# A two-layer encoder on one core: the order of the last products of a group of pairs, and which engine copies one of their sums

## The chip, the core and the metric

The kernel runs on one core of a Trainium2 chip. Its engines work beside each other, each through its own queue of instructions in a fixed order: TensorE (PE, with its weight loads shown as PEld) multiplies matrices and adds into PSUM; VectorE (DVE) and ScalarE (ACT) read and write PSUM and the on-chip memory SBUF; GpSimd (POOL) and SyncE (SP) only issue transfers here. An instruction waits until those whose results it reads, or whose data it overwrites, are done. The metric is the device time of one execution in microseconds (us).

## The reference

Two layers over 512 tokens and 16 learned ones (528 columns in the kernel, 512 in the last block), 1024 channels, in float32:

```python
for l in range(DEPTH):
    h = h + 0.5 * swiglu(rmsnorm(h, norm_gains[l, 0]),
                         ffn_w_gate[l, 0], ffn_w_up[l, 0], ffn_w_down[l, 0])
    h = h + mixer(rmsnorm(h, norm_gains[l, 1]), ...)
    h = h + 0.5 * swiglu(rmsnorm(h, norm_gains[l, 2]),
                         ffn_w_gate[l, 1], ffn_w_up[l, 1], ffn_w_down[l, 1])
return rmsnorm(h, final_norm)[:, N_META:]

def swiglu(x, w_gate, w_up, w_down):
    return (jax.nn.silu(x @ w_gate) * (x @ w_up)) @ w_down
```

The mixer (gated linear attention beside softmax attention) isn't touched by the change. The four `swiglu` blocks are, each with 2816 hidden channels.

## The kernel before, in words

**Two parts of each number.** Every matrix product is made in three: each operand is split into a high part (a cast to the type that TensorE multiplies fast) and a low part (what the cast left). High times high, high times low and low times high add up in PSUM. The high part of a block of weights is a cast on ScalarE (line 287), the low part a subtraction on VectorE (line 288). Activations are split likewise (lines 673 and 674 for the down products).

**Seven products for eight.** In the feed-forward blocks the products are made by a scheme of the Strassen kind: operands are cut in two each way, and seven products of sums and differences replace eight. They are named "1" to "7". Products 1, 6, 7 and 4 of a pair add up in one PSUM tile (X), product 2 has one of its own (Y), products 5 and 3 share a third (Z). "Pair" means two blocks of 128 hidden channels, with gate and up; there are 11 in a feed-forward block, in groups of 4, 4 and 3. One product of a pair is 24 matmuls of 264 columns (256 in the last block), all at line 598.

The running sum in X is read after each product, and the next one then adds on: ScalarE copies it out after products 1, 6 and 7 (`snapshot`, line 602); VectorE adds Y or Z to the copies (lines 608, 618, 625). `hidden` then multiplies by the norm's factor (line 642), applies the activation on ScalarE (line 444) and multiplies gate and up (line 652).

**A group's end.** Behind the last pair of each of the first two groups (pairs 3 and 7) the hidden channels of the group, four pairs of them, are multiplied by the down weights, again in seven products ("S" steps, `fast_down`, matmuls at line 712, sums added to the result `h` at line 720), for each of two halves of the output. Their operands are made from the four hidden quarters by `operand` (lines 673 and 674) and `difference` (line 678). As three of the four pairs are done early, the first operands are made in two steps ("O"): three quarters while the last pair is still at work, the last quarter behind it. So the first three down products of the first half have a part 1 (18 matmuls, for three pairs) and a part 2 (6, for the last pair). There are two such places in each of four blocks, eight in all.

**Weights.** They come through SP's queue in blocks of 128 x 1024 into three buffers, or for sums into others; products 3, 5, 6 and 7 need sums or differences of weight blocks, which are made by transfers of POOL's queue that add to what is there (line 208), by VectorE (line 256) or begin with a negated copy on ScalarE (line 203). `W.behind` keeps a cast of weights behind the last copy of a sum on ScalarE's queue. Blocks are fetched nine loads ahead and split three ahead, in the order of their use.

The order of the steps is written out in `ffn_steps`; a scheduler then places each engine's instructions, so that their order on an engine can differ a little from that of the code.

Of the kernel before, what the change touches and what calls it, by code (L numbers as in the profile page):

```python
# [14 lines left out]
ALU = mybir.AluOpType  # L15
AX = mybir.AxisListType

P = 128
# [22 lines left out]

GROUPS = (4, 4, 3)
FAST = 2
QUADS = 2
LATE = 5
HELD = 4
# [6 lines left out]
def ffn_steps(opening):  # L53

    steps, pair = [], 0
    for g, n in enumerate(GROUPS):

        ahead = g == 0  # L60
        begun = 0 < g <= FAST
        steps += [("P", p, c) for p in range(pair, pair + 1 + ahead) for c in "12"] * (not begun)
        early4 = (0, 1) if opening and ahead else ()
        steps += [("P", p, "4") for p in early4]
        steps += [("P", pair, c) for c in "65"] * (not begun)
        for i in range(n):
            p, more = pair + i, i + 1 < n
            early = [[("P", p + 1, "1")], [("P", p + 1, "2")]] if more else \
                [[("D", g, 0, 0, 2 * n - 2)], [("D", g, 1, 0, 2 * n - 2)]]
            if ahead and i == 0:  # L70
                early = [[], []]
            if not more and g < FAST:
                rest = [("S", g, 0, c, 2) for c in "125"]
                steps += [("O", g, 0), ("P", p, "7"), ("P", p, "4"), ("S", g, 0, "1", 1), ("P", p, "3")]
                steps += [("S", g, 0, c, 1) for c in "25"] + [("O", g, 1)] + rest
                turns = [("S", g, *t, 3) for t in zip(AB, "16273465734")]
                steps += turns[:6]
                for s, c in zip(turns[6:], "1265"):
                    steps += [s, ("P", p + 1, c)]
                steps.append(turns[-1])  # L80
                continue
            steps += early[0] + [("P", p, "7")] + early[1] + [("P", p, c) for c in "43" if c == "3" or p not in early4]
            if more:
                steps += [("P", p + 1, "6"), ("P", p + 1, "5")]
        if g >= FAST:
            steps += [("D", g, m, 0, 2 * n - 2) for m in range(2, HELD)]
            steps += [("D", g, m, 2 * n - 2, 2 * n) for m in range(HELD)]
            steps += [("D", g, m, 0, 2 * n) for m in range(HELD, KC)]
        pair += n
    return steps  # L90
# [238 lines left out]
def build(tc, ctx, xt, wts, win, par, w2, const, umask, out):  # L329
# [243 lines left out]
    def ffn(l, f, norm, done, following):  # L573
# [7 lines left out]
        def product_of_pair(p, product):  # L581
            kind = "s2" if p % 2 == 0 else "ss"
            st = made.setdefault(p, {})
            apart = product == "4" and "r" not in st
            where, begin = {"1": ("X", 1), "6": ("X", 0), "7": ("X", 0), "4": ("X", 0), "2": ("Y", 1), "5": ("Z", 1),
                            "3": ("Z", 0)}[product]
            if apart:
                where, begin = "W", 1
            if begin:
                st[where] = pair(kind == "s2")  # L590
            acc = st[where][:, :, :w]

            hi, lo = W.op((l, f), p, product, ahead=AHEAD_MADE - 1)
            at = PLACE[product]
            for k, (xh, xl) in enumerate(x):
                for j in range(2):
                    for i, (a, b) in enumerate(((hi, xh), (hi, xl), (lo, xh))):
                        TE.matmul(acc[:, j], a[:, j, k], b[:, at], start=bool(begin and k == 0 and i == 0),  # L598
                                  stop=k == len(x) - 1 and i == 2, skip_group_check=not begin)

            def snapshot(q):
                W.behind = S.copy(part(st, q), acc).ins  # L602

            if product == "1":
                st["c"] = [c_tile() for _ in range(2)]
                snapshot(0)
            elif product == "2":
                V.tensor_tensor(part(st, 0), part(st, 0), acc, ALU.add)
            elif product == "6":
                snapshot(1)  # L610
            elif apart:
                S.copy(part(st, 2), acc)
                st["apart"] = True
            elif product == "7":
                snapshot(3)
                if "apart" in st:
                    V.tensor_tensor(part(st, 2), part(st, 2), part(st, 3), ALU.add)
                V.tensor_tensor(part(st, 3), part(st, 3), st["Z"][:, :, :w], ALU.add)
                st["r"] = True
                if "apart" in st:  # L620
                    hidden(st, p, 1)
            elif product == "4":
                hidden(st, p, 1)
            elif product == "3":
                V.tensor_tensor(part(st, 1), part(st, 1), acc, ALU.add)
                hidden(st, p, 0)
# [121 lines left out]
        for i, step in enumerate(steps):  # L748
# [16 lines left out]
            elif step[0] == "O":  # L765
                g, last = step[1:]
                ks = slice(3, 4) if last else slice(0, 3)
                operands_of(g, ks, "215" if last else "125")
                difference(g, 0, 3, 0, ks)
                if last:  # L770
                    operand(g, "6")
# [599 lines left out]
```

## Time and profile before

| what | value |
|---|---|
| median of 3 runs | 2212.42 us (2210.72 to 2214.04) |
| the profiled execution | 2211.05 us |
| its span, first to last instruction | 2209.2 us |
| PE busy | 2162.4 us, 98% |
| VectorE busy | 1785.4 us, 81% |
| ScalarE busy | 1214.1 us, 55% |
| POOL busy | 101.8 us, 5% |
| granted TensorE clock, mean | 0.997 |

A row of a timeline has the start and the duration in us, the engine, the line, the operation, what is written and read, the shape, and a count where instructions follow each other; behind them, in brackets, the engine's idle time ahead of it and what ended it. A row of the view of waits has the waiting engine with its line, what it waited for, and the total in us, the number and the longest. A matmul's duration overlaps with the next one's, so distances are taken from start to start. The tile names are the program's: `ss` is a PSUM sum, `xc` an activation operand, `whi` and `wlo` the parts of a block of weights, `w`, `s` and `raw` blocks or sums of weights, `c` a pair's copies (or an operand of the down products), `g` a hidden quarter or an operand, `h` the result.

### The profile page before, as it was taken

The page shows a single profiled execution, that of the slowest core. Times are in us where ns is not written, and L with a number is a line of the kernel's source. Part 1 is how long each engine was busy: PE and PEld are TensorE (multiplying, and loading weights), DVE is VectorE, ACT ScalarE, POOL GpSimd, SP SyncE. Part 2 cuts the span into 40 slices and gives each one's busy share as a digit, 9 for nine tenths or more (in the row PEclk, how much of TensorE's full clock was granted, in tenths as well). Part 3 has the DMA queues.
Part 4 walks back from the last instruction along what each step waited for, and adds up shares of the span by engine and source line. Part 5 has one row for each costly group of instructions (what it writes and reads, how often), then busy time and mean ns, then how long its engine had stood idle before and what let it go on. Part 6 is the DMA issues. An engine that isn't in the chain of part 4 may idle for free.

```text
span 2209.2 us, 40079 instructions
## 1 busy us (share of the span) xinstructions
PE 2162.4 (98%) x16506; PEld 2070.2 (94%) x16506; DVE 1785.4 (81%) x2703; ACT 1214.1 (55%) x1779; POOL 101.8 (5%) x120
## 2 busy tenths in 40 slices
PE   7999999999999999999999999999999999999998
PEld 6999999989999999999999999999788888999997
DVE  7897978486886689889789979775879767997987
ACT  7544545344785555454575445453457836554543
POOL 1000000000000001000010000000000001000100
PEclk9999999999999999999999999999999999999999
DMA  9775753212113468666567757432121145776752
GB/s 268 189 204 160 191 152 106 82 49 68 49 39 122 114 167 205 190 182 187 162 163 186 207 164 191 143 110 77 49 84 51 42 133 152 198 202 181 189 165 67
DMA packets 87463, 311.41 MB, mean 141 GB/s; under 512 B 9712, under 2 KB 12144, under 8 KB 87280
## 3 DMA queue, kind: packets, MB, share of 16 engines
q1 hardware_dynamic: 68624, 245.53, 32.9%
q0 software_dynamic: 16704, 60.82, 15.8%
q8 instruction: 130, 2.13, 0.4%
q10 hardware_dynamic: 1952, 2.50, 0.4%
q14 instruction: 53, 0.43, 0.1%
HBM read 289.94 MB, written 2.10 MB: 132 GB/s over the span
## 4 chain that ended last, share of the span: by engine, by line
PE 81%; DVE 11%; ACT 4%; issue 2%; DMA 2%; SPq 0%; DVEq 0%; ACTq 0%
PE ss L598 37%; PE mm L465 13%; PE ss L712 11%; PE ss L465 10%; PE sm L465 2%; DVE wlo L288 2%; DMA w<-win 2%; PE sm L1074 1%; PE ss L1049 1%; DVE g L678 1%; ACT whi L287 1%; PE sm L1090 1%; DVE h L720 1%; PE ss L471 1%; PE sm L1091 1%
## 5 line engine op out<-in xcount | busy, mean ns | idle before, releaser
L598 PE MATMUL ss<-xc,whi 128*128 128x264 f32 (+1 forms) x4928 | 907.2, 285 | 15.5 <-ACT whi L287 7.4
L598 PEld LDWEIGHTS ss<-xc,whi 128*128 128x128 f32 x4928 | 767.2, 189 | 20.4 <-ACT c L602 8.4
L598 PE MATMUL ss<-xc,wlo 128*128 128x264 f32 (+1 forms) x2464 | 702.5, 285 | 8.8 <-DVE wlo L288 8.8
L598 PEld LDWEIGHTS ss<-xc,wlo 128*128 128x128 f32 x2464 | 466.5, 189 | 11.1 <-DVE wlo L288 10.9
L288 DVE TENSOR_TENSOR wlo<-w,whi 128x1024 fp32r<-128x1024 f32 (+1 forms) x337 | 408.1, 1217 | 63.4 <-ACT whi L287 63.2
L287 ACT CAST whi<-w 128x1024 fp32r<-128x1024 f32 (+1 forms) x337 | 350.0, 1050 | 163.3 <-PE ss L598 80.5
L465 PE MATMUL mm<-x,whi 128*128 128x264 f32 (+1 forms) x1712 | 384.6, 315 | 0.0
L465 PEld LDWEIGHTS mm<-x,whi 128*128 128x128 f32 x1712 | 278.3, 188 | 16.5 <-issue 1.0
L465 PE MATMUL mm<-x,wlo 128*128 128x264 f32 (+1 forms) x856 | 266.0, 315 | 0.0
L712 PE MATMUL ss<-g,whi 128*128 128x264 f32 (+1 forms) x1280 | 237.4, 284 | 0.0
L287 ACT CAST whi<-raw 128x1024 fp32r<-128x1024 f32 x126 | 132.3, 1050 | 163.4 <-PE mm L465 102.3
L602 ACT COPY c<-ss 128x528 f32<-128x528 f32 (+1 forms) x132 | 78.5, 594 | 258.6 <-PE ss L598 258.6
L288 DVE TENSOR_TENSOR wlo<-raw,whi 128x1024 fp32r<-128x1024 f32 x126 | 153.9, 1222 | 59.0 <-ACT whi L287 58.1
L712 PEld LDWEIGHTS ss<-g,whi 128*128 128x128 f32 x1280 | 198.4, 188 | 0.1
L712 PE MATMUL ss<-g,wlo 128*128 128x264 f32 (+1 forms) x640 | 181.3, 283 | 0.0
L465 PEld LDWEIGHTS mm<-x,wlo 128*128 128x128 f32 x856 | 159.6, 188 | 8.5 <-issue 0.7
L465 PE MATMUL ss<-g,whi 128*128 128x264 f32 (+2 forms) x900 | 166.3, 299 | 0.0
L465 PEld LDWEIGHTS ss<-g,whi 128*128 128x128 f32 x900 | 131.7, 188 | 5.3
L208 POOL DMA_DIRECT2D w<-win x60 | 52.7, 878 | 1574.7 <-DVE wlo L288 582.5
L712 PEld LDWEIGHTS ss<-g,wlo 128*128 128x128 f32 x640 | 120.5, 188 | 0.0
L444 ACT ACTIVATE c<-c 128x528 f32<-128x528 f32 (+1 forms) x88 | 56.6, 643 | 98.5 <-DVE c L642 98.4
L465 PE MATMUL ss<-g,wlo 128*128 128x264 f32 (+2 forms) x450 | 106.2, 300 | 0.0
(267 smaller groups left out, 3370.2 us busy)
## 6 DMA issues: line engine op xcount, KB each, us to landing
w<-win SPq DMA_DIRECT2D x335, 512.0 KB, 4.5
raw<-wts SPq DMA_DIRECT2D x126, 512.0 KB, 3.3
w<-win POOLq DMA_DIRECT2D x60, 512.0 KB, 7.4
s<-win POOLq DMA_DIRECT2D x24, 512.0 KB, 7.2
w<-s POOLq DMA_DIRECT2D x24, 512.0 KB, 5.6
s<-w POOLq DMA_DIRECT2D x8, 512.0 KB, 9.6
h<-xt SPq DMA_DIRECT2D x3, 528.0 KB, 6.8
out<-h ACTq DMA_DIRECT2D x4, 256.0 KB, 2.4
```

Source lines behind the costliest of these rows:

```text
L208: self.nc.gpsimd.dma_start(t, src, accum_op=ALU.add)
L287: nc.scalar.copy(hi[:, cs], w[:, cs])
L288: nc.vector.tensor_tensor(lo[:, cs], w[:, cs], hi[:, cs].bitcast(F32), ALU.subtract)
L444: prev_act[0] = S.activation(*args, **kw).ins
L465: TE.matmul(acc.half[i][:width], lhs, rhs[:, acc.spans[i]], start=first, stop=last)
L471: TE.matmul(a, weights, x[:, hs], start=True, stop=True)
L598: TE.matmul(acc[:, j], a[:, j, k], b[:, at], start=bool(begin and k == 0 and i == 0), stop=k == len(x) - 1 and i == 2, skip_group_check=no ...
L602: W.behind = S.copy(part(st, q), acc).ins
L678: V.tensor_tensor(r[into][:, ks], r[a][:, ks], r[b][:, ks], ALU.subtract)
L712: TE.matmul(acc[:, j], a[:, j, k], xs[b][:, k], start=bool(begin and k == 0 and i == 0), stop=k == 3 and i == 2, skip_group_check=not begin)
L720: V.tensor_tensor(to, to, acc, ALU.add)
L1049: TE.matmul(s[:n, i, :HF], lhs, kh[:, hs], start=True, stop=False)
```

## The change

In the last pair of the first two groups three things are moved. The third product comes ahead of the fourth, with part 1 of the first down product between them. The fifth product's sum (Z) is copied by ScalarE when it is complete, and the seventh's sum (X) is then added to that copy by VectorE; before, ScalarE copied X behind product 7 and VectorE added Z. And the first down products of the first half come in the order first, fifth, second instead of first, second, fifth, in both parts; their operands are made in that order.

```diff
+LAST = [sum(GROUPS[: g + 1]) - 1 for g in range(FAST)]
...
             if not more and g < FAST:
-                rest = [("S", g, 0, c, 2) for c in "125"]
-                steps += [("O", g, 0), ("P", p, "7"), ("P", p, "4"), ("S", g, 0, "1", 1), ("P", p, "3")]
-                steps += [("S", g, 0, c, 1) for c in "25"] + [("O", g, 1)] + rest
+                rest = [("S", g, 0, c, 2) for c in "152"]
+                steps += [("O", g, 0), ("P", p, "7"), ("P", p, "3"), ("S", g, 0, "1", 1), ("P", p, "4")]
+                steps += [("S", g, 0, c, 1) for c in "52"] + [("O", g, 1)] + rest
...
+            elif product == "5":
+                if p in LAST:
+                    snapshot(3)
+            elif product == "7" and p in LAST:
+                V.tensor_tensor(part(st, 3), part(st, 3), acc, ALU.add)
+                st["r"] = True
...
-                operands_of(g, ks, "215" if last else "125")
+                operands_of(g, ks, "152")
```

The instructions of every engine are as many as before; at each of the eight places they stand in another order. In the rows below a name has its number and an allocation number; line numbers of the changed kernel are 1 higher up to line 615 of the old one and 7 higher behind it. `whi188` is the high part of weight block 188, and so on; `w22_01_3` is block 22 of the weights of layer 0, second feed-forward block, pair 3. `ss814` is X of pair 3, `ss818` its Z.

On PE, at the first group's end in the second block of layer 0: from the end of product 7 (block 187) to the products behind it, before.

```order
L598 MATMUL ss814_9836<-xc787_9210,wlo187_10012 128x264
L712 MATMUL ss825_10163<-g819_10078,whi189_10092 128x264
L712 MATMUL ss825_10163<-g820_10079,whi189_10092 128x264
L598 MATMUL ss814_9836<-xc754_8778,whi188_10049 128x264
...
L598 MATMUL ss814_9836<-xc787_9210,wlo188_10050 128x264
L712 MATMUL ss825_10163<-g819_10078,wlo189_10093 128x264
...
L598 MATMUL ss818_10048<-xc754_8778,whi190_10129 128x264
```

The same place in the change, from the end of product 7 on.

```order
L599 MATMUL ss814_9836<-xc787_9210,wlo187_10012 128x264
L599 MATMUL ss818_10048<-xc754_8778,whi188_10049 128x264
...
L599 MATMUL ss818_10048<-xc787_9210,wlo188_10050 128x264
L719 MATMUL ss825_10162<-g819_10079,whi189_10093 128x264
...
L599 MATMUL ss814_9836<-xc754_8778,whi190_10129 128x264
```

Behind product 7, which writes `ss814`, comes a product that writes `ss818`; the one that adds to `ss814` again comes behind the first down product's part 1.

On ScalarE, at the same place, before: from the copy behind product 6 to the activations.

```order
L602 COPY c815_9868<-ss814_9836 128x2x264
L287 CAST whi188_10049<-w22_01_3_9842 128x1024
L673 CAST g821_10082<-g806_9506 128x792
L673 CAST c823_10087<-g804_9504 128x792
L287 CAST whi189_10092<-w11_01_11_9875 128x1024
L602 COPY c816_9869<-ss814_9836 128x2x264
L287 CAST whi190_10129<-s4_01_3_9944 128x1024
L287 CAST whi191_10164<-w12_01_11_9946 128x1024
L203 ACTIVATE s3_01_12_10226<-w11_01_12_10015 128x1024
L287 CAST whi192_10186<-w21_01_11_9879 128x1024
L444 ACTIVATE c816_9869<-c816_9869 128x528
```

And in the change.

```order
L603 COPY c815_9866<-ss814_9836 128x2x264
L288 CAST whi188_10049<-s4_01_3_9944 128x1024
L680 CAST g823_10088<-g806_9506 128x792
L603 COPY c816_9867<-ss818_10048 128x2x264
L680 CAST c821_10084<-g804_9504 128x792
L288 CAST whi189_10093<-w11_01_11_9873 128x1024
L288 CAST whi190_10129<-w22_01_3_9913 128x1024
L288 CAST whi191_10163<-w21_01_11_9877 128x1024
L288 CAST whi192_10185<-w12_01_11_9980 128x1024
L204 ACTIVATE s3_01_12_10226<-w11_01_12_10015 128x1024
L445 ACTIVATE c815_9866<-c815_9866 128x528
```

The copy of `ss814` behind product 7 is gone; a copy of `ss818` stands two instructions earlier, ahead of the cast of the fifth operand (`c823` before, `c821` now) and of block 189. The negated copy for the next half's sums (`s3_01_12`) now stands behind four casts and directly ahead of the first activation.

On VectorE, at the same place, before: from the add behind product 7 to the last quarter of the first operand.

```order
L618 TENSOR_TENSOR c816_9869<-c816_9869,ss818_10048 128x2x264
...
L256 TENSOR_TENSOR s4_01_11_10253<-w22_01_11_9877,w12_01_11_9946 128x1024
L674 TENSOR_TENSOR g822_10083<-g806_9506,g821_10082 128x264
L625 TENSOR_TENSOR c815_9868<-c815_9868,ss818_10048 128x2x264
L642 SCALAR_TENSOR_TENSOR c815_9868<-c815_9868,rs800_9428 128x528
L288 TENSOR_TENSOR wlo193_10223<-w11_01_12_10015,whi193_10222 128x1024
L652 TENSOR_TENSOR g804_9504<-c815_9868 128x264
L652 TENSOR_TENSOR g805_9505<-c815_9868 128x264
L674 TENSOR_TENSOR g820_10079<-g804_9504,g819_10078 128x264
L678 TENSOR_TENSOR g804_9504<-g805_9505,g804_9504 128x264
```

And in the change.

```order
L619 TENSOR_TENSOR c816_9867<-c816_9867,ss814_9836 128x2x264
L289 TENSOR_TENSOR wlo190_10130<-w22_01_3_9913,whi190_10129 128x1024
L632 TENSOR_TENSOR c815_9866<-c815_9866,ss818_10048 128x2x264
L289 TENSOR_TENSOR wlo191_10164<-w21_01_11_9877,whi191_10163 128x1024
L649 SCALAR_TENSOR_TENSOR c815_9866<-c815_9866,rs800_9428 128x528
...
L659 TENSOR_TENSOR g804_9504<-c815_9866 128x264
...
L681 TENSOR_TENSOR g820_10080<-g804_9504,g819_10079 128x264
L681 TENSOR_TENSOR g824_10089<-g806_9506,g823_10088 128x264
L685 TENSOR_TENSOR g804_9504<-g805_9505,g804_9504 128x264
```

The third product's sum (`c815`, line 625 before and 632 now) is added two instructions behind the seventh's instead of ten, and a weight split stands between it and the multiply that reads it (line 642, now 649).

On SP's queue the loads of `w22_01_3` and `w11_01_11` change places, and with them their buffers; on POOL's queue the accumulating transfers for the second half's fifth and sixth weight sums (`w21_01_12`, `w22_01_12`) change places.

## The prediction

> **What bounds the kernel now.** The page comes first: which engine is full.
>
> ```profile
> PE 2162.4 (98%) x16506; PEld 2070.2 (94%) x16506; DVE 1785.4 (81%) x2703; ACT 1214.1 (55%) x1779; POOL 101.8 (5%) x120
> ```
>
> TensorE (PE) is busy for 98% of the span, so the number of matmuls sets the time, and the change leaves that number alone. What it can move is PE's idle time. The view of waits, for PE and its weight loads (PEld), tells which of it lies at the change:
>
> ```profile
> PE ss L598 <- ACT c L602: 6.1, 11, 0.7
> PE ss L712 <- DVE c L674: 3.4, 8, 0.6
> PEld ss L712 <- DVE c L674: 7.2, 16, 0.8
> ```
>
> L598 is a product of a pair, L602 ScalarE's copy of a sum out of PSUM, L712 a first down product, L674 the low part of its operand. Eight waits are one for each group end (two groups in each of four feed-forward blocks); sixteen are two for each. The timeline of PE at one group end (layer 0, second block, first group), which I use as the pattern, shows all three:
>
> ```profile
> 858.18 0.40 PE L712 MATMUL ss<-g,whi 128*128 128x264 f32 x2
> 859.08 0.51 PE L598 MATMUL ss<-xc,whi 128*128 128x264 f32 x2 [0.50 <-ACT c L602]
> ...
> 872.83 0.73 PE L712 MATMUL ss<-c,whi 128*128 128x264 f32 x2
> 873.40 0.28 PE L712 MATMUL ss<-c,wlo 128*128 128x264 f32 x1
> ...
> 876.94 0.41 PE L712 MATMUL ss<-g,whi 128*128 128x264 f32 x2
> 877.73 0.39 PE L712 MATMUL ss<-c,whi 128*128 128x264 f32 x1 [0.39 <-DVE c L674]
> ```
>
> Two matmuls that don't wait take 0.245 us from start to start (24 of them 2.94, by the chain row quoted below). From the starts, the fourth product loses 859.08 - 858.18 - 0.245 = 0.655 us, since it adds to the PSUM bank that ScalarE still copies; the second part of the fifth down product loses 873.40 - 872.83 - 0.245 = 0.325; the sixth loses 877.73 - 876.94 - 0.245 = 0.545. With some 0.1 for each restart it is about 1.7 us, 14 us over eight places. But between these waits VectorE (DVE) has no room. The view by windows, from the low part of weight block 188 to the last operand, here and at the two places of the last block, whose tiles are 256 columns wide instead of 264:
>
> ```profile
> core 0: us, PE busy (x) PEld busy (x) DVE busy (x) ACT busy (x) POOL busy (x), PEclk, DMA share, GB/s
> 855.04:876.42 21.38, 20.81 (x169) 20.39 (x168) 20.90 (x31) 14.09 (x18) 3.08 (x4) 1.00 0.89 213
> 1932.41:1953.35 20.94, 20.32 (x170) 19.92 (x170) 20.62 (x31) 14.03 (x18) 3.39 (x4) 1.00 0.87 215
> 2053.47:2074.28 20.81, 20.28 (x170) 19.88 (x170) 20.57 (x30) 14.05 (x18) 2.77 (x4) 1.00 0.90 222
> ```
>
> DVE is busy for 20.90 of 21.38 us. Whatever PE saves at the fourth product, it meets the sixth down product's operand, which comes at the end of DVE's queue. So a group end is a DVE stage inside a PE kernel, and the gain is what DVE gains.
>
> **The change part by part.** *The wait at the fourth product.* ScalarE now copies the fifth product's sum, which is complete one product earlier; the seventh product's sum is added to it by DVE straight from PSUM, and the third product, which writes another bank, goes between. The same number of copies and adds is left. The third product's weights are ready: DVE ends the low part of block 188 by 855.04 + 1.22 = 856.26, and the seventh product ends at 858.3. PE's 0.655 + 0.1 goes: 8 x 0.755 = 6.0 us, if nothing behind it takes it back. The fourth product then starts behind the third and the first down product's first part, 24 + 18 matmuls or 5.1 us later (863.4), long after the DVE add that it has to wait for.
>
> *What DVE gets back.* The 31 instructions stay, in the same sizes. These are their starts in the timeline of DVE, where the stage runs late:
>
> ```profile
> 866.51 0.43 DVE L674 TENSOR_TENSOR g<-g,g 128x264 fp32r<-128x264 f32 x1
> 867.18 0.70 DVE L625 TENSOR_TENSOR c<-c,ss 128x528 f32<-128x528 f32 x1 [0.24 <-PE ss L598]
> 867.92 0.71 DVE L642 SCALAR_TENSOR_TENSOR c<-c,rs 128x528 f32<-128x528 f32 x1
> 869.68 0.77 DVE L652 TENSOR_TENSOR g<-c 128x264 f32<-128x264 f32 x2
> 870.59 0.43 DVE L674 TENSOR_TENSOR g<-g,g 128x264 fp32r<-128x264 f32 x1
> 871.06 1.73 DVE L678 TENSOR_TENSOR g<-g,g 128x264 f32<-128x264 f32 x2
> 872.70 0.43 DVE L674 TENSOR_TENSOR c<-g,c 128x264 fp32r<-128x264 f32 x1
> 873.04 0.70 DVE L720 TENSOR_TENSOR h<-h,ss 128x528 f32<-128x528 f32 x1
> 873.66 1.22 DVE L288 TENSOR_TENSOR wlo<-w,whi 128x1024 fp32r<-128x1024 f32 x1
> 876.42 1.26 DVE L674 TENSOR_TENSOR c<-g,c 128x1056 fp32r<-128x1056 f32 x1
> ```
>
> Where the next instruction is ready, a 264-column one takes 0.34 from start to start (872.70 to 873.04) and a 528-column one 0.62 (873.04 to 873.66). Against that four places are long. L674 to L625: 0.67, so 0.33 too much, since DVE waits for the third product to end. L625 to L642, which reads its result: 0.74, 0.12 too much. Two L652 to L674: 0.91 against 0.68, 0.23 too much, for the cast of ScalarE. L674 to L678: 0.47, 0.13 too much. In the new order the third product ends at 858.3 + 2.94 = 861.2 and DVE comes to its sum at 861.7, behind the seven instructions that begin at 855.04; a weight split stands between that sum and the multiply that reads it; the cast for the first operand has some 3 us; and another low part stands between the first operand's and the difference that overwrites its source. All four go: 0.33 + 0.12 + 0.23 + 0.13 = 0.81, and the last operand is ready at 877.68 - 0.81 = 876.87. PE would be there 24 + 3 matmuls behind the second down product's part, at 876.3, and waits 0.6 instead of 0.545. The gain of the place is 0.81, not 1.7.
>
> On dependent instructions the Trainium skill says otherwise ("VectorE: DVE Perf Modes", section "The DRAIN you can't avoid"): the next operation does not start before the pipe is empty, and a semaphore in between costs nothing extra, so setting dependent instructions apart would save nothing. By it the place would gain 0.56. The rows disagree, 0.74 beside 0.62 for instructions of one size, and I go by the rows.
>
> *What ScalarE (ACT) is asked for.*
>
> ```profile
> 855.18 0.86 ACT L673 CAST c<-g 128x792 fp32r<-128x792 f32 x1
> 855.94 1.05 ACT L287 CAST whi<-w 128x1024 fp32r<-128x1024 f32 x1
> 858.43 0.60 ACT L602 COPY c<-ss 128x528 f32<-128x528 f32 x1 [1.44 <-PE ss L598]
> ...
> 860.83 1.06 ACT L203 ACTIVATE s<-w 128x1024 f32<-128x1024 f32 x1
> ...
> 875.31 1.08 ACT L673 CAST c<-g 128x1056 fp32r<-128x1056 f32 x1 [0.16 <-DVE g L678]
> 883.41 1.05 ACT L287 CAST whi<-w 128x1024 fp32r<-128x1024 f32 x1 [0.61 <-PE ss L712]
> ```
>
> The copy moves from 858.43, behind 1.44 us of idle time, to the end of the fifth product at 855.5; there it waits 0.3 and then holds the cast of the fifth operand and that of weight block 189 back by 0.8. DVE wants them at 857.07 and 857.96; they are done at 856.85 and 857.80. So the move is free by some 0.2 us, the thinnest cover here: were each of two steps 0.25 later than that, the gain would be 0.3 instead of 0.81.
>
> *Loads.* SP's queue swaps two loads that come far ahead of use. But the load for the next block's first weight (block 193, also the source of L203) now goes into the buffer that weight block 189 leaves, not 188: it is issued at 859.2 instead of 856.29. Landing times of this load and the next at this place, of the next at the last block's first place, and of one that shared the DMA engines with a POOL transfer (us at the row's end):
>
> ```profile
> w<-win SPq DMA_DIRECT2D x1, 512.0 KB, 4.5
> w<-win SPq DMA_DIRECT2D x1, 512.0 KB, 3.6
> w<-win SPq DMA_DIRECT2D x1, 512.0 KB, 6.3
> w<-win SPq DMA_DIRECT2D x1, 512.0 KB, 7.4
> 856.29 0.33 SPq L198 DMA_DIRECT2D w<-win  x1
> ```
>
> At 3.6 it lands at 862.8, and ACT, which comes to L203 at 862.5 behind four weight casts, loses 0.3; the activation behind it ends at 864.9, and DVE wants it at 865.3. Every landing up to 5.1 costs less than the gain. I take 3.6, since in the new order no other load is under way then, and one place in five as late as 6.3: there it costs 2.0.
>
> *POOL* swaps two accumulating transfers per place. The fifth weight sum, cast behind L203's 860.83 before, is now wanted at 858.7, behind blocks 189 and 190; it was issued at 849.54 and landed 7.0 later, 856.5. The sum of sixth weights, now behind the other, lands some 3 us later than 868.29 + 7.6 = 875.9, and is cast at 883.41 less 0.8.
>
> ```profile
> 849.54 0.86 POOL L208 DMA_DIRECT2D w<-win  x1 [2.64 <-DVE g L652]
> 868.29 0.87 POOL L208 DMA_DIRECT2D w<-s  x1 [5.12 <-DMA s<-win]
> w<-win POOLq DMA_DIRECT2D x1, 512.0 KB, 7.0
> w<-s POOLq DMA_DIRECT2D x1, 512.0 KB, 7.6
> 864.22 2.94 PE ss L598 x24
> ```
>
> *The sum.* Six places at 0.81, and the two of the last block, whose DVE idles 0.16 and 0.24 less in its window (0.32 and 0.24 against 0.48), at 0.6: 4.9 + 1.2 = 6.1. Less 0.2 x 2.0 for late loads: 5.7. Between places PE has work in every slice, so the gain reaches the end. The profiled execution took 2211.05 us; it becomes 2205.4. The median of the runs shown is 2212.42, 1.4 above it, so I forecast 2206.7.
>
> **The rivals.**
> *The gain mostly doesn't come (same).* New small stalls of DVE behind ACT's later casts, or dependent instructions that cost the same wherever they stand, leave 0.3 to 0.5 a place: 2.4 to 4, so 2208.4 to 2210. For it: covers of only 0.2 us on ACT. Against: DVE's four long steps are visible, and each has its reason removed. 0.2% is 4.4 us, about what a measurement tells from no change. Chance 0.24; the skill's rule on the pipe is a case of this (8 x 0.56 = 4.5, less 0.4), with 0.04 of it, for the row speaks against it.
>
> *The late load (slower).* If the load for block 193 lands 7.4 us after 859.2, at 866.6, L203 ends at 867.7 and the activation at 868.3; DVE stands from 865.3 on, 3.0 us, and loses 2.2 a place net: 17.6, so 2230. It decides from a landing of 5.1 on. For it: landings up to 7.4 beside POOL's transfers. Against: this one starts when the load before it has landed. The Trainium skill ("DMA: Bandwidth & Descriptors", section "Issuing engines are not separate DMA queues") has transfers of all queues share the same 16 DMA engines; the trace agrees, 7.4 beside a POOL transfer and 3.6 nearly alone. Chance 0.07.
>
> *PE's waits all go (faster by more).* If DVE's order freed the last operand early, 1.7 x 8 = 13.6 would go: 2198.8. Against it stands DVE's 20.90 us of work. Chance 0.05.
>
> **How the numbers follow.** The forecast, 2205 to 2208, has 0.64. Faster by more than 0.2%: 0.64 + 0.05 less a little for its upper edge, 0.67; same 0.25; slower 0.08. The range leaves out most of the late load and of the last rival and takes in the small gains: 2202 to 2211.5.
>
> **What would show it.** In the profile after: no wait of PE for a copy at the eight group ends (the eleven become three); the wait for the sixth operand still there, near 0.6; the last operand some 0.8 earlier behind the end of the seventh product than 18.1 us; no idle time of DVE at the third product's sum. Wrong would be a DVE wait on the activation with ACT waiting for a load ahead of it, or PE waits at the fifth down product, which now comes before the second.

## The result, and the profile after

The changed kernel takes 2205.64 us (median, 2203.49 to 2207.16), the one before 2212.73 us on the same chip: a ratio of 0.9969, 95% interval 0.9957 to 0.9981. The forecast was 2206.7 us, and faster. Measured once more beside other kernels the ratio was 0.9968 (0.9956 to 0.9981). The profiled execution took 2203.49 us, with a span of 2201.6, 7.6 less than before.

The view of waits after the change, whose lines answer to those of L598 and L712 before (the product of a pair is now L599, a first down product L719, ScalarE's copy L603, the low part L681):

```profile
PE ss L599 <- DVE wlo L289: 8.5, 8, 4.7
PE ss L719 <- DVE c L681: 3.4, 8, 0.6
PE ss L599 <- ACT c L603: 2.1, 3, 0.7
```

Of eleven waits for a copy three are left, and the sixth operand is still waited for at all eight places. The same stage, from the low part of weight block 188 to the last operand, by windows (the columns are those of the prediction's fence):

```profile
851.66:872.24 20.58, 20.54 (x169) 20.33 (x168) 20.55 (x31) 14.20 (x18) 2.61 (x3) 1.00 0.80 200
```

The first stage went from 21.38 to 20.58 us, by 0.80, and VectorE is now busy for 20.55 of it: its 0.48 us without work shrank to 0.03, and its busy time by 0.35, with the same 31 instructions, since more of them begin before the one ahead has ended. In the timeline of VectorE no row of this stage has an idle time in brackets:

```profile
858.37 0.70 DVE L632 TENSOR_TENSOR c<-c,ss 128x528 f32<-128x528 f32 x1
858.98 1.22 DVE L289 TENSOR_TENSOR wlo<-w,whi 128x1024 fp32r<-128x1024 f32 x1
860.12 0.70 DVE L649 SCALAR_TENSOR_TENSOR c<-c,rs 128x528 f32<-128x528 f32 x1
...
861.87 0.77 DVE L659 TENSOR_TENSOR g<-c 128x264 f32<-128x264 f32 x2
862.56 0.43 DVE L649 SCALAR_TENSOR_TENSOR c<-c,rs 128x264 f32<-128x264 f32 x1
...
866.20 0.77 DVE L681 TENSOR_TENSOR g<-g,g 128x264 fp32r<-128x264 f32 x2
866.88 1.72 DVE L685 TENSOR_TENSOR g<-g,g 128x264 f32<-128x264 f32 x2
...
870.61 0.43 DVE L685 TENSOR_TENSOR g<-g,g 128x264 f32<-128x264 f32 x1
870.96 1.31 DVE L727 TENSOR_TENSOR h<-h,ss 128x528 f32<-128x528 f32 x2
872.24 1.26 DVE L681 TENSOR_TENSOR c<-g,c 128x1056 fp32r<-128x1056 f32 x1
```

The third product's sum (L632) follows with no wait and is left after 0.61. The two multiplies of gate and up (L659) take 0.69 (861.87 to 862.56), where the pair took 0.91 before. Two low parts (L681) take 0.68 until the difference begins (866.20 to 866.88), 0.34 each, where one took 0.47 before. And PE at the end of the stage:

```profile
872.76 0.41 PE L719 MATMUL ss<-g,whi 128*128 128x264 f32 x2
873.55 0.39 PE L719 MATMUL ss<-c,whi 128*128 128x264 f32 x1 [0.39 <-DVE c L681]
```

PE loses 873.55 - 872.76 - 0.245 = 0.545 there, to the hundredth what it lost before: it comes 0.8 earlier, and so does the operand. The prediction measured the way from the end of product 7, near 858.3, to the last operand, 18.1 us; counted from the start of the last matmul of product 7, it was 18.36 before at this place and is 17.55 now.

What each place gained can be read off PE: the two kernels issue the same number of matmuls, so the start of the matmul with the same number, before less after, is taken ahead of a place and behind it. The differences are 0.78, 0.80, 0.86, 0.86, 0.81, 0.84 at the six places of 264 columns, and 0.05 and 0.54 at the last block's two: 5.54. Between the places they stay within 0.15, and add up to 0.3. The remaining 1.75 us of the spans' difference of 7.6 lie ahead of the first place, where both kernels have the same instructions.

### The profile page after: what moved, and what is told of

Same layout as the page of the kernel before. It is cut to its first block, busy times and chain, and to the rows that moved or that the text cites. A ratio compares the mean times of both kernels' runs of the same rounds, so it can differ in the third digit from the quotient of the medians.

```text
span 2201.6 us, 40079 instructions
## 1 busy us (share of the span) xinstructions
PE 2158.9 (98%) x16506; PEld 2068.2 (94%) x16506; DVE 1782.3 (81%) x2703; ACT 1213.6 (55%) x1779; POOL 101.7 (5%) x120
## 4 chain that ended last, share of the span: by engine, by line
PE 74%; DVE 16%; ACT 4%; issue 2%; DMA 2%; SPq 0%; DVEq 0%; ACTq 0%
PE ss L599 32%; PE mm L466 13%; PE ss L719 11%; PE ss L466 10%; DVE wlo L289 4%; PE sm L466 2%; DMA w<-win 2%; DVE g L685 1%; PE sm L1081 1%; DVE c L681 1%; DVE g L681 1%; DVE c L649 1%; DVE g L659 1%; PE ss L1056 1%; ACT whi L288 1%
## 5 line engine op out<-in xcount | busy, mean ns | idle before, releaser
L599 PE MATMUL ss<-xc,whi 128*128 128x264 f32 (+1 forms) x4928 | 904.4, 285 | 11.4 <-ACT whi L288 7.5
L599 PEld LDWEIGHTS ss<-xc,whi 128*128 128x128 f32 x4928 | 765.9, 189 | 14.4 <-ACT whi L288 7.7
L599 PE MATMUL ss<-xc,wlo 128*128 128x264 f32 (+1 forms) x2464 | 701.7, 285 | 8.7 <-DVE wlo L289 8.5
L599 PEld LDWEIGHTS ss<-xc,wlo 128*128 128x128 f32 x2464 | 465.9, 189 | 10.9 <-DVE wlo L289 10.7
L719 PE MATMUL ss<-g,whi 128*128 128x264 f32 (+1 forms) x1280 | 237.2, 284 | 0.1
L603 ACT COPY c<-ss 128x528 f32<-128x528 f32 (+1 forms) x132 | 78.6, 595 | 244.3 <-PE ss L599 244.0
L719 PEld LDWEIGHTS ss<-g,whi 128*128 128x128 f32 x1280 | 198.5, 188 | 0.4 <-DVE g L681 0.3
L719 PE MATMUL ss<-g,wlo 128*128 128x264 f32 (+1 forms) x640 | 181.3, 283 | 0.0
L719 PEld LDWEIGHTS ss<-g,wlo 128*128 128x128 f32 x640 | 120.4, 188 | 0.0
```

The source lines that it names most:

```text
L719: TE.matmul(acc[:, j], a[:, j, k], xs[b][:, k], start=bool(begin and k == 0 and i == 0), stop=k == 3 and i == 2, skip_group_check=not begin)
```

## The experiments

Each edit is shown against the changed kernel. "Places" is the sum of the eight gains, measured as above against the profile before; "ahead" is the offset at the first place.

| kernel | median, us | before beside it | ratio (95%) | places | ahead |
|---|---|---|---|---|---|
| changed, first time | 2205.64 | 2212.73 | 0.9969 (0.9957 to 0.9981) | 5.54 | 1.75 |
| changed, again | 2203.73 | 2210.82 | 0.9968 (0.9956 to 0.9981) | 5.34 | -1.70 |
| copy alone | 2216.96 | 2210.54 | 1.0029 (1.0017 to 1.0040) | -5.99 | 0.30 |
| order alone | 2211.53 | 2210.54 | 1.0001 (0.9993 to 1.0010) | -0.82 | -0.19 |
| down products back | 2205.27 | 2210.54 | 0.9975 (0.9965 to 0.9984) | 6.08 | -1.41 |
| more for VectorE | 2216.20 | 2210.82 | 1.0022 (1.0013 to 1.0031) | -6.59 | -0.61 |
| more for ScalarE | 2206.13 | 2210.82 | 0.9979 (0.9970 to 0.9988) | 5.07 | -0.12 |
| sixth operand first | 2202.51 | 2210.54 | 0.9962 (0.9950 to 0.9975) | 8.82 | -0.17 |
| seventh's difference late | 2209.42 | 2210.82 | 0.9995 (0.9986 to 1.0004) | 4.31 | -0.43 |
| operands one step earlier | 2199.39 | 2210.64 | 0.9954 (0.9940 to 0.9968) | 13.54 | -1.46 |

The last two columns of "more for VectorE" are from its single later run (2217.77 us).

The theory is the prediction's: a group's end is as long as VectorE's queue up to the sixth operand. The rival was that the gain is PE's own: the wait for the copy is taken away, and that is all. The result alone can't tell them apart. A matmul that doesn't wait takes PE 0.1225 us (2.94 for 24). What PE needs beyond that at the third place adds up to 1.74 us before and 0.96 after, and the part that went is the 0.76 at the fourth product; but VectorE's stage too became shorter, by 0.80.

**The changed kernel again.** Nothing is edited.

> The changed kernel itself once more, beside the experiments of this call. If the 7.6 us between the two profiled spans hold 1.75 us of start-up that differ by chance (ahead of the first group end, where both kernels have the same matmuls), the first group end is reached at another offset here, and the places again give 0.8 each at six places and 0.5 to 0.65 at the two of the last block: 5.5 to 6.1 in the places. If the start-up belongs to the change, the offset of 1.75 is there again. In the last block's first place the gain was 0.05 beside a load that landed after 4.92 us: with a landing under 4.2 it should be 0.5 or more.

The places gave 0.79, 0.81, 0.81, 0.79, 0.81, 0.81, 0.00 and 0.52. The start-up did not belong to the change: the offset ahead of the first place was 1.75 in one profile of this kernel and -1.70 in the other. The waits show 2.0 of these 3.45 us. Six of the eight waits in this row lie in the first 100 us; it is the row of the second profile, beside 8.5 in the first:

```profile
PE ss L599 <- DVE wlo L289: 10.5, 8, 5.0
```

The places thus give 5.3 to 5.5 us. The medians differ by 7.1, and the interval of the first measurement, 4.2 to 9.5 us, holds both; that the rest is chance is not shown. In the last block's first place the load for the next weights landed late again, 4.97 us after its issue. What it does is told under the reasons below.

**One part alone: the copy.** The edit takes the old order back and leaves the copy where the change puts it:

```diff
-                steps += [("O", g, 0), ("P", p, "7"), ("P", p, "3"), ("S", g, 0, "1", 1), ("P", p, "4")]
-                steps += [("S", g, 0, c, 1) for c in "52"] + [("O", g, 1)] + rest
+                steps += [("O", g, 0), ("P", p, "7"), ("P", p, "4"), ("S", g, 0, "1", 1), ("P", p, "3")]
+                steps += [("S", g, 0, c, 1) for c in "25"] + [("O", g, 1)] + rest
...
-                operands_of(g, ks, "152")
+                operands_of(g, ks, "215" if last else "125")
```

(`rest` goes back to "125" as well.)

> The changed kernel with only the copy moved (ScalarE copies the fifth product's sum, VectorE adds the seventh's from PSUM); the fourth product again right behind the seventh, and the down products and their operands in the old order. Theory of the prediction (VectorE's queue is the limit of a group end): the fourth product now has to wait for VectorE's add of the seventh's sum, which stands behind two weight splits and ends some 2.4 us after the seventh product; the third product, and VectorE's add of its sum, come 1.7 us later than before the change, so a place costs about 1.6 us more than before the change: 2225, slower than before (2212.7). Rival (the gain is simply that PE no longer waits for ScalarE's copy): that wait is gone here too, 8 x 0.755, so about 2206.7, as fast as the whole change.

It is slower, as the theory has it, against the rival; but by 6.4 us and not by 12, and by another way. The fourth product does have to wait until VectorE has read X (the add starts at 860.74), but the scheduler filled most of that time with the first down product, PE's rows L719 between matmuls of the pair (L599):

```profile
859.51 0.51 PE L599 MATMUL ss<-xc,whi 128*128 128x264 f32 x2 [0.17 <-ACT whi L288]
859.99 0.39 PE L719 MATMUL ss<-g,wlo 128*128 128x264 f32 x1
...
861.71 0.41 PE L599 MATMUL ss<-xc,whi 128*128 128x264 f32 x2
```

PE loses 0.66 us around these rows, where the wait for the copy took 0.76 before. So that wait is gone, but its time is not saved, and this kernel doesn't test the rival as it was meant to. What made the six places of 264 columns 0.89 to 0.99 us longer (the last block's two 0.17 and 0.22) stands in VectorE's timeline. In the scheduler's order the weight split that before stood between the multiply and the activation's reader now comes ahead of the multiply (868.93), and so nothing covers the activation:

```profile
860.74 0.70 DVE L619 TENSOR_TENSOR c<-c,ss 128x528 f32<-128x528 f32 x1
...
865.81 1.22 DVE L289 TENSOR_TENSOR wlo<-w,whi 128x1024 fp32r<-128x1024 f32 x1 [0.28 <-ACT whi L288]
...
868.93 1.22 DVE L289 TENSOR_TENSOR wlo<-w,whi 128x1024 fp32r<-128x1024 f32 x1
870.07 0.70 DVE L649 SCALAR_TENSOR_TENSOR c<-c,rs 128x528 f32<-128x528 f32 x1
871.49 0.78 DVE L659 TENSOR_TENSOR g<-c 128x264 f32<-128x264 f32 x2 [0.71 <-ACT c L445]
```

The stage by windows, from the low part of block 188 to the last operand as before:

```profile
855.79:878.17 22.38, 21.93 (x173) 21.04 (x171) 21.02 (x30) 14.35 (x19) 3.27 (x4) 1.00 0.87 209
```

It is 1.00 us longer than before the change (22.38 against 21.38): VectorE stands without work for 1.36 instead of 0.48, most of it the 0.71 and the 0.28 above, and is busy 0.12 longer. The place lost 0.99. So VectorE's lost time went into the time one to one, as the theory has it, though my sum for this kernel was wrong.

**The other part alone: the order.** The copy's branches are left out:

```diff
-            elif product == "5":
-                if p in LAST:
-                    snapshot(3)
-            elif product == "7" and p in LAST:
-                V.tensor_tensor(part(st, 3), part(st, 3), acc, ALU.add)
-                st["r"] = True
```

> The changed kernel with only the order changed: third product ahead of the fourth, down products first, fifth, second, but ScalarE again copies the seventh product's sum and VectorE adds the fifth's to it. Theory of the prediction: the third product writes the bank that VectorE still has to read behind that copy, so it starts some 2.4 us after the seventh product instead of 0.9; PE comes to the sixth down product 20.1 us or more after the end of the seventh product instead of 19.4: some 0.9 us a place, about 2220, slower than before. Rival (the order carries the gain, since VectorE's long steps go with it): 0.8 a place gained, 2206.5.

No change, where slower was expected and faster by the rival. The third product cannot start, so the scheduler puts the first down product ahead of it; and that finds its weights' low part not yet made, which in the whole change is needed one product (2.94 us) later:

```profile
861.96 0.39 PE L713 MATMUL ss<-g,wlo 128*128 128x264 f32 x1 [1.54 <-DVE wlo L289]
```

At the stage's end PE has no wait left. VectorE's low part of the sixth operand ends at 878.65 (877.40 + 1.25), and the sixth product starts 0.76 later:

```profile
879.41 0.48 PE L713 MATMUL ss<-c,whi 128*128 128x264 f32 x2
```

So VectorE's queue is as short here as in the whole change, and PE itself is late: one wait of 1.54 in place of the three it replaces makes this place 0.15 longer. The theory holds only where PE gets to the sixth product before its operand. Neither half of the change is worth anything alone.

**The order of the down products.** Only their order is taken back:

```diff
-                steps += [("S", g, 0, c, 1) for c in "52"] + [("O", g, 1)] + rest
+                steps += [("S", g, 0, c, 1) for c in "25"] + [("O", g, 1)] + rest
...
-                operands_of(g, ks, "152")
+                operands_of(g, ks, "215" if last else "125")
```

> The changed kernel with the first down products and their operands back in the order first, second, fifth; copy and third product as changed. Theory of the prediction: VectorE has the same instructions ahead of the sixth operand, its four long steps stay gone, so the same time as the changed kernel, 2205.6, within 1.5. Rival (part of the gain is the fifth down product's operand, which PE waited 0.33 for at each place and which now comes in another place of the order): 0.3 x 8 lost, 2208.

The same as the changed kernel, as far as the intervals tell: 0.80 to 0.86 at the six places. No worth of the third part of the change is seen; VectorE has the same instructions ahead of the sixth operand either way.

**More work for VectorE.** The low part of the second operand is written twice:

```diff
-                V.tensor_tensor(lo, src[:, ks], hi.bitcast(F32), ALU.subtract)
+                for _ in range(2 if c == "2" and ks == slice(0, 3) else 1):
+                    V.tensor_tensor(lo, src[:, ks], hi.bitcast(F32), ALU.subtract)
```

> The changed kernel with more work for VectorE in each group end: the low part of the second down product's operand (792 columns) is written twice, with the same values; the planner then also puts one weight split (1024 columns) ahead of the sixth operand. PE and ScalarE have no more to do. Theory of the prediction (VectorE is the limit of the stage): 0.89 + 1.14 = 2.0 us later at each place, 12 to 16 us for six to eight places: 2218 to 2222. Rival (the gain came from PE's own order, VectorE had room): 2205.6, within 1.5.

It ended 2216.2 beside 2210.8, where the changed kernel was 2203.7: 12 us (by the ratios) for 0.9 us more of VectorE and one split put forward, at each place. Of the 12 us, 2.0 are one late load, told below. The same kernel once more, for its profile:

> The kernel with VectorE's doubled low part once more, for its profile. Theory of the prediction: no idle time of VectorE between the doubled low part and the sixth operand, and PE waits for the sixth operand 1.5 us or more longer at each place than in the changed kernel (0.39 in the rows). Rival: the loss is a wait of PE for another product's operand or weights.

The sixth operand came 2.3 us later behind the first down product than in the changed kernel (16.8 against 14.5), PE lost 1.29 to 1.38 of that at six of the places (the scheduler had put more matmuls ahead). None of it shows as a wait for the sixth operand's low part; PE waits instead for the adds to `h`, 0.6 at a time, which stand in the same late queue and read PSUM sums that PE needs free.

```profile
PE ss L720 <- DVE h L728: 4.7, 8, 0.8
```

So the expectation of a longer wait for the sixth operand missed, and its rival, a wait for something else, is what the rows show. What they wait for is late in VectorE's queue all the same: more work for VectorE, with none added to PE, makes the place longer. One place, the third, lost 3.40 against the changed kernel, some 2.0 more than the others. There the load for the next weights landed after 5.48 us, and the chain that the prediction had as its slower rival can be seen whole, in ScalarE's and VectorE's timelines:

```profile
867.48 1.06 ACT L204 ACTIVATE s<-w 128x1024 f32<-128x1024 f32 x1 [4.26 <-DMA w<-win]
868.44 0.63 ACT L445 ACTIVATE c<-c 128x528 f32<-128x528 f32 x1
...
869.10 0.78 DVE L659 TENSOR_TENSOR g<-c 128x264 f32<-128x264 f32 x2 [1.91 <-ACT c L445]
```

**More work for ScalarE.** The moved copy is made twice:

```diff
             elif product == "5":
                 if p in LAST:
                     snapshot(3)
+                    snapshot(3)
```

> The changed kernel with the moved copy of the fifth product's sum made twice by ScalarE (0.49 us more at each place, behind the cast of the fifth operand and ahead of that of weight block 189). Theory of the prediction (the cover of ScalarE is some 0.2 us): VectorE waits 0.3 us for the cast of block 189 at each place, 2.4 in all: 2208. Rival (ScalarE has room at a group end): the same as the changed kernel, 2205.6, within 1.

The six places gave 0.66 to 0.74 instead of 0.78 to 0.86, and the last 0.40 instead of 0.54: some 0.12 less, where 0.3 was expected. (The seventh gave 0.51; its load landed after 3.48 us.) VectorE's queue shows where: a difference starts 1.01 behind the low part, where a step between independent instructions of that size takes 0.89; the scheduler put it in front of the split that the late cast holds.

```profile
855.71 0.97 DVE L682 TENSOR_TENSOR c<-g,c 128x792 fp32r<-128x792 f32 x1
856.72 0.98 DVE L686 TENSOR_TENSOR g<-g,g 128x792 f32<-128x792 f32 x1
857.62 1.22 DVE L289 TENSOR_TENSOR wlo<-w,whi 128x1024 fp32r<-128x1024 f32 x1
```

So the loss is the 0.12 of a step that overwrites what the step ahead of it reads, and no idle time. By ScalarE's timeline the cast of block 189 is the first of three from 855.84, of 0.95 each, and ends near 856.8; in the old order VectorE would have wanted it at 856.60, and waited the 0.2 to 0.3 that was expected. The scheduler filled that hole, so the run bounds what the cover is worth (0.12 a place), not the cover.

**The sixth operand first.** If the sixth operand's place in the queue is what PE waits for, giving it priority must pay:

```diff
-                difference(g, 0, 3, 0, ks)
-                if last:
-                    operand(g, "6")
+                with tc.high_priority() if last else nullcontext():
+                    difference(g, 0, 3, 0, ks)
+                    if last:
+                        operand(g, "6")
```

> The changed kernel, but the difference, cast and low part of the sixth down product's operand get priority: ScalarE casts it ahead of one weight block, VectorE takes its difference ahead of one weight split and its low part ahead of one add to h. Theory of the prediction (VectorE's and ScalarE's place for this operand is what PE waits for at the end of a group): the operand is ready 0.65 us earlier, PE's 0.55 us at each of eight places goes: 2205.6 - 4.4 = 2201.2. Rival (the next thing is just as late: the weight split behind it, or the following operands): the wait moves on by one or two products, 2204 to 2206.

At the six places the gain rose from 0.8 to 1.22 to 1.28, and the wait is gone there; at the last block's two the scheduler left the old order, and the wait stayed. The rows are the wait and, for the third place, VectorE's queue with the difference ahead of the split and the low part behind one add instead of two:

```profile
PE ss L719 <- DVE c L681: 0.9, 2, 0.5
```

```profile
870.68 0.42 DVE L685 TENSOR_TENSOR g<-g,g 128x264 f32<-128x264 f32 x1
871.02 1.22 DVE L289 TENSOR_TENSOR wlo<-w,whi 128x1024 fp32r<-128x1024 f32 x1
872.16 0.69 DVE L727 TENSOR_TENSOR h<-h,ss 128x528 f32<-128x528 f32 x1
872.77 1.25 DVE L681 TENSOR_TENSOR c<-g,c 128x1056 fp32r<-128x1056 f32 x1
```

The places give 3.3 to 3.5 us more than the changed kernel's, where 4.4 was expected. Only 2.6 to 2.7 of that are the edit's, some 0.45 at each of six places; the other 0.7 come at the seventh place, where the order is the old one and the load happened to land early (3.52 us). The intervals of the two ratios overlap, so the places show this gain and the times do not.

**The seventh operand's difference late.** On top of that, 1.2 us of VectorE's work ahead of the fifth and sixth operands are held back:

```diff
                 S.copy(hi, src[:, ks])
-                V.tensor_tensor(lo, src[:, ks], hi.bitcast(F32), ALU.subtract)
+                made[("low", g, c)] = V.tensor_tensor(lo, src[:, ks], hi.bitcast(F32), ALU.subtract).ins
...
-                difference(g, 1, 1, 3)
+                with after(made["low", g, "6"]):
+                    difference(g, 1, 1, 3)
                 operand(g, "7")
```

> The kernel with the sixth operand first, and also the difference for the seventh operand (1056 columns, 1.2 us of VectorE) held back behind the sixth operand's low part. Theory of the prediction (what stands ahead of an operand in VectorE's queue is what PE waits for): the remaining 0.2 us for the fifth operand at six places and 0.5 us for the sixth at the two places of the last block go as well: 1.1 + 1.1 less than with the sixth operand first alone, 2200.3. Rival (the seventh operand, now later, is waited for instead): 2202.5 or more.

The rival held. The six places gave 0.91 to 0.96 instead of the 1.22 to 1.28 above, the last two -1.05 and -0.30, and 2.5 us were lost between the places. Only the order on VectorE's queue changed, and the wait moved on, to low parts of later operands (the first row, twelve of them), and in the last block to a weight cast that stands behind a late transfer:

```profile
PE ss L720 <- DVE g L681: 3.9, 12, 0.4
PE ss L720 <- ACT whi L288: 3.5, 2, 2.2
```

**The operands one step earlier.** The sixth operand first, and:

```diff
-                steps += [("S", g, 0, c, 1) for c in "52"] + [("O", g, 1)] + rest
+                steps += [("S", g, 0, "5", 1), ("O", g, 1), ("S", g, 0, "2", 1)] + rest
```

> The kernel with the sixth operand first, and the last quarter of all operands issued one step earlier in the program (behind the fifth down product's first part instead of the second's). In the planner's order the fifth operand's low part then comes ahead of the seventh's difference, and the sixth's low part ahead of a weight split and one or two adds to h, at the two places of the last block too. Theory of the prediction: the waits of 0.2 us for the fifth operand at six places and of 0.5 us for the sixth at the last two go, 2.0 in all, while nothing stands behind them as the seventh operand did: 2200.5. Rival (each operand that comes earlier makes another late, as in the run before): 2202.5 or more.

This has the lowest median, 2199.39 us, 0.9954 of before, some 3 us below the changed kernel by the ratios; but the intervals overlap, and its five runs fall into two groups, three near 2199.4 and two near 2203.2. PE has no wait for the sixth operand at any place; the gain is 1.68 to 1.81 at six places and 1.62 and 1.46 at the last two. Of these 13.5 us, 3.95 are lost again between the places. Of that, 1.76 lies between the second place and the third, a stretch in which the other kernels' offsets too moved by -1.39 to 0.75; the rest, 0.1 to 0.6 behind each place, goes at least in part into a new wait, again for a low part in VectorE's queue:

```profile
PE ss L719 <- DVE g L681: 1.9, 7, 0.4
```

So its median came out lower than expected although something else did become late. I have not followed the rest of the 3.95.

## Why the prediction was right

*That VectorE is the limit.* Right, and shown from both sides: 1.00 us more in VectorE's stage (the copy alone) made a place 0.99 longer, more work on VectorE cost 1.3 a place, and a shorter queue ahead of the sixth operand gained 0.45 a place without touching the wait for the copy. The way from the start of product 7's last matmul to the start of the sixth operand's low part shows it place by place, in the six places of 264 columns:

| kernel | way, us | change against before | gain of the place |
|---|---|---|---|
| before | 18.34 to 18.37 | | |
| changed | 17.55 to 17.57 | -0.78 to -0.82 | 0.78 to 0.86 |
| copy alone | 19.26 to 19.35 | +0.91 to +0.99 | -0.89 to -0.99 |
| down products back | 17.55 | -0.79 to -0.82 | 0.80 to 0.86 |
| more for ScalarE | 17.67 to 17.68 | -0.66 to -0.70 | 0.66 to 0.74 |

In these kernels PE still waits for that operand, and the gain is the way's change to within 0.1 us at every place. In the order alone the way is 17.48 to 17.52, PE doesn't wait for the operand, and the place gains nothing. The rival that all of PE's waits go fell with the 0.545 still standing.

*The 0.81 of a place.* Measured 0.78 to 0.86 in one profile, 0.79 to 0.81 in the other. All four long steps went. The term by the Trainium skill's rule ("VectorE: DVE Perf Modes", section "The DRAIN you can't avoid"), 0.56, is not what came. The prediction took only half of that section: it also says that a next operation that is not held starts earlier, and the 0.61 below for independent instructions of 0.70 each agrees with that. Other kernels show the price of a dependent step by itself: in the order alone the third product's sum and the multiply that reads it are 0.73 apart (866.19 to 866.92), in the changed kernel the same sum and a weight split behind it 0.61; and the 0.12 of the doubled copy above is the same price.

```profile
866.19 0.69 DVE L626 TENSOR_TENSOR c<-c,ss 128x528 f32<-128x528 f32 x1
866.92 0.71 DVE L643 SCALAR_TENSOR_TENSOR c<-c,rs 128x528 f32<-128x528 f32 x1
```

*The 0.6 of the last block's places.* Right for the second (0.54, 0.52), and 0.65 and 0.53 with the down products back. Wrong for the first, 0.05 and 0.00: the late load. The row is ScalarE's, with the wait that it hands on to VectorE:

```profile
1934.63 1.06 ACT L204 ACTIVATE s<-w 128x1024 f32<-128x1024 f32 x1 [2.09 <-DMA w<-win]
...
1936.25 0.76 DVE L659 TENSOR_TENSOR g<-c 128x256 f32<-128x256 f32 x2 [0.51 <-ACT c L445]
```

*The late load's term.* The mechanism was right; the sum and the limit were not. One place in five at 2.0 us each is 3.2 us over eight places, not the 0.4 that was taken off: by its own rate the sum is 2.9 and the forecast 2209.5, still inside the range. Measured, it took one place of eight, at 0.5, in both profiles, so that 0.4 came near is luck. And "every landing up to 5.1 costs less than the gain" was worked out for a place of 264 columns, which has 0.8 to lose. In the last block a landing of 4.92 and 4.97 took the whole 0.54, while 3.56 (down products back), 3.52 (sixth operand first) and 3.48 (more for ScalarE) left 0.65, 0.73 and 0.51. At 264 columns 4.33 cost nothing (0.81 in the second profile), and 5.48 some 2.0 beside the other places, in a kernel that issues the load later. I have not varied the load by itself: that it is the cause rests on these rows, in which the landing and the loss go together.

Why it lands late can be followed in the trace. While it is under way (the window 1929.6 to 1934.8 of the first profile), one packet of 16 KB of another queue passes, which the profile names instruction. The row has the number of packets, the MB and the share of the 16 DMA engines' time:

```profile
q8 instruction: 1, 0.02, 1.2%
```

The load ends with 16 packets of 4 bytes. In the first profile of the changed kernel 15 of them come by 1932.65 and the last one only at 1934.16; the packet of the instruction queue lies at 1932.39 to 1933.39, ahead of it. The second profile is the same (1935.88 and 1937.45; 1935.72 to 1936.68). In the three kernels with a landing near 3.5 the packet starts within 0.01 us of the end of the load's last one (1932.51 with the sixth operand first). So it is most likely a matter of which of the two comes first on one DMA engine; the trace does not name a packet's engine, so that they share one is inferred. The landings at 4.11 and 4.33 (a packet of 0.96 and 1.27 us right at the issue) and at 5.48 (one of 2.38) have such a packet too; at other places one passes and the load is not late.

*ScalarE's cover.* No cost of moving the copy is seen, as forecast; with 0.49 us more work on ScalarE the cover named (0.2 us) would have been used up by the rows, but the scheduler's other order on VectorE left only 0.12 of loss.

*POOL's swap and SP's.* No other wait for a transfer took time from a place. Of the two signs of being wrong, ScalarE waiting for a load and VectorE for its activation came at one place, the seventh; PE's wait at the fifth down product is what it was, 0.30 (868.68 to 869.23 in the third place) against 0.325.

*The sum.* 5.7 forecast, 5.54 and 5.34 in the places; with the late load's term at its own rate it would have been 2.9. Of the 7.6 us between the spans 1.75 are start-up in favour of the profile after, which a second profile of the same kernel has the other way round.

*The other rival.* That the gain mostly wouldn't come (0.3 to 0.5 a place) did not happen; the small new stalls that it needed are not in the rows.

## What to carry to other kernels

Where one engine is 98% busy, look for the short stages in which another one's queue ends last; there a wait of the busy engine that is removed is met again at the end of the stage, unless that queue gets shorter, and its idle and dependent steps are the gain to count. Two halves of a reordering can each be worthless while the whole pays: here the scheduler's order for each half left a hole elsewhere, 0.88 us more idle time of VectorE in one, a wait of PE of 1.54 us in the other. And before a difference of spans is explained, take the offset of the same instruction ahead of the first changed place: here 1.75 of 7.6 us was the start-up.

## What was not expected of the hardware

The start-up, with the same instructions, differs by up to 3.45 us between two executions of one kernel (1.75 and -1.70 against the same profile before). One load of 512 KB, issued at the same point of the program about when the transfer ahead of it lands, took 3.1 to 3.6 us at six of the eight places in both profiles of the changed kernel, 4.11 and 4.33 at the sixth, and 4.92 and 4.97 at the seventh. At the seventh all but one of its 16 last packets were there 1.5 us before the last, beside one packet of the instruction queue that took 1.0 us.
